# A two-layer diffusion trunk on one core: the latents' tables beside the context's mixer, layer 1's preparations behind it, and one tile's V rows summed on TensorE

## The chip, the core and the metric

One core of a Trainium2 chip (trn2) runs the whole program. The metric is the time of one execution in device microseconds (us); lower is better. The core has five engines that each work through a list of instructions of their own, in a fixed order, and wait for each other by semaphores: TensorE (PE in the profile; its weight loads are PEld), VectorE (DVE), ScalarE (ACT), GpSimd (POOL) and SyncE (SP). DMA transfers are issued by SP (all plain ones here) and by POOL (the gathers and a few loads), and run on 16 DMA engines.

## The reference

Two layers, each a token mixer and then a PEER feed-forward block, on 512 latent tokens and 256 context tokens of width 1024. In layer 0 the context is updated too; layer 1 needs the context only as input.

```python
for layer in range(2):
    y, yc = token_mixer(modulate(rms_norm(x)), modulate(rms_norm(xc)), ...)   # attention, Hyena, S5, gated merge
    x = x + g1 * y
    x = x + g2 * peer_ffn(modulate(rms_norm(x)), wq, sub_keys, u_tab, v_tab)
    if layer == 0:
        xc = xc + mc2 * yc
        xc = xc + mc5 * peer_ffn(modulate(rms_norm(xc)), wq, sub_keys, u_tab, v_tab)

def peer_ffn(x, ...):                       # 8 heads, 128 x 128 = 16384 experts, 16 chosen per head and token
    s = einsum('thsk,hsnk->thsn', x @ wq, sub_keys)       # scores against two halves of the key
    best, expert = top 16 of the sums of the two halves' top 16
    act = gelu(einsum('td,thkd->thk', x, u_tab[expert]))
    return einsum('thk,thkd->td', softmax(best) * act, v_tab[expert])
```

## The kernel before

Each part of the work is a Python generator that emits instructions and yields a cost; `weave` takes several of them, each with a factor, and always advances the one whose sum of cost times factor is least. A factor is thus a pace: a greater one means fewer steps in the same stretch. The order that comes out is fixed at build time for each engine, and an engine whose next instruction waits holds up all that stand behind it. Layer 0's middle is one such weave and then a second, smaller one.

The first weave holds five chains. (1) The context's mixer (`ctx_rest`, banks `pm`): attention, Hyena, S5, merge; its end is marked "c1". Behind it in the same chain comes `ctx_side`: the context's norm, its scores (16 projections) and for each of its two tiles of 128 tokens the pick of 128 experts per token (`peer_pick`, all on VectorE: maxima, indices, one-hot sums), after which ids and weights stand ready ("ids", q). (2) `peer_u` (banks `pu`): 128 **U tiles**, each of which loads 512 KB of the U table, splits it into a high and a low part (`wh` on ScalarE, `wl` on VectorE), multiplies it with all 512 latents in 24 matmuls of 512 columns and writes 256 KB of activations to memory. It runs until "tabs" is marked, in groups of eight; U tiles that are then left are done in the V stage. Its factor is 10 until "c1", 1.2 after it. (3) `aside` (banks `ps`): the latents' norm, layer 1's preparations `s5_prep` and `hy_prep`, the latents' scores, and for the four latent tiles a pick and then a dense gate table (`peer_table`: one-hot matrices `ohA`, `ohB` on VectorE, matmuls, 1 MB writes `ge`). When the fourth table is out it marks "tabs". (4) `gather`: for each context tile, 128 indirect DMAs of 128 rows of U (tile `gx`, 512 KB each, issued by POOL), each followed by one dot product on VectorE (L1198), then 128 gathers of V rows, each followed by one multiply-and-add on VectorE (L170). It needs the pool "gx", which `aside` opens after "c1". Its factor is 1.69. (5) `mods`, layer 1's modulation vectors, whose matmuls have 32 output rows and stand four side by side in one bank.

The second weave is the **V stage**: `peer_v` (banks `pa`, `px`) takes 128 steps; each loads 512 KB of the V table and 256 KB of activations, reads a share of the gate tables, splits both factors and does 24 matmuls of 512 columns. What is left of `gather` runs beside it with the factor 1.5; what is left even then goes on beside layer 1.

## Time and profile before

| | |
|---|---|
| median of the runs shown (3) | 5627.69 us (5614.76 to 5642.93) |
| the profiled execution's own time | 5628.3 us |
| its span, first to last instruction | 5626.4 us |
| busy over the span: PE, DVE, ACT, POOL | 87%, 66%, 31%, 26% |
| mean granted clock of TensorE | 0.932 of 2.4 GHz |
| DMA over the span | 1333.39 MB, 237 GB/s |

Busy shares are unions of an engine's instructions in time. The clock has two levels, 1.2 and 2.4 GHz; a mean between them says what share of the time stood at which. "DMA share" is the mean busy share of the 16 DMA engines. The context's mixer stands at about 890 to 1530 us of the span, the rest of the first weave reaches to 2545, the V stage to 3412, layer 1 to the end.

### The profile page before, as it was taken

How to read it: one execution, taken by the hardware profiler on the slowest of the kernel's cores; microseconds unless marked ns; L12 is line 12 of the kernel's file. 1: busy time of each engine (PE TensorE's matmuls, PEld its weight loads, DVE VectorE, ACT ScalarE, POOL GpSimd, SP SyncE). 2: the span in 40 equal slices, each digit the busy share in tenths (PEclk: the TensorE clock that was granted, in tenths of full speed). 3: DMA queues.
4: the chain of work that ended last, by engine and by line, in shares of the span. 5: the costliest groups of instructions: out<-in, count | busy, mean ns of one | idle time of the engine just before them, and what ended most of it. 6: DMA issues, size and time to landing. Idle time of an engine off the chain costs nothing.

```text
span 5626.4 us, 72472 instructions
## 1 busy us (share of the span) xinstructions
PE 4889.1 (87%) x25801; PEld 4010.3 (71%) x25801; DVE 3728.4 (66%) x7594; ACT 1758.3 (31%) x2651; POOL 1442.0 (26%) x1626
## 2 busy tenths in 40 slices
PE   6888878869997889998888887999889899998886
PEld 5666557648886777786766676875578899897665
DVE  5643426644499899987777775544345989776777
ACT  3221524314442322332222224334233333332322
POOL 0003500000002344443444441406000111243333
PEclk9899989879998999999989998999899999999998
DMA  6557335666556889899999896562444676788897
GB/s 208 190 186 262 110 111 179 206 200 189 184 175 207 303 280 325 312 329 343 324 321 321 311 308 219 174 216 75 144 148 154 214 255 240 261 311 297 310 320 257
DMA packets 641795, 1333.39 MB, mean 237 GB/s; under 512 B 56438, under 2 KB 342391, under 8 KB 626329
## 3 DMA queue, kind: packets, MB, share of 16 engines
q1 hardware_dynamic: 522776, 871.53, 47.2%
q0 software_dynamic: 118656, 457.23, 23.0%
q8 instruction: 203, 3.33, 0.2%
q14 instruction: 160, 1.30, 0.1%
HBM read 1147.01 MB, written 181.49 MB: 236 GB/s over the span
## 4 chain that ended last, share of the span: by engine, by line
PE 26%; DMA 14%; DVE 12%; issue 9%; POOL 4%; ACT 1%; SPq 1%; DVEq 0%; POOLq 0%; ACTq 0%
PE pa L181 6%; PE ps L181 5%; PE two L181 5%; DMA gx<-in_peer_v_dram,t 3%; POOL gx L1185 3%; DMA va<-t 3%; PE pu L181 3%; PE px L181 3%; PE pm L181 2%; PE pf L181 2%; DMA gt<-t 2%; DMA t<-ge 2%; DVE t L170 2%; DVE wl L160 2%; DMA x<-in_peer_v_dram 1%
## 5 line engine op out<-in xcount | busy, mean ns | idle before, releaser
L160 DVE TENSOR_TENSOR wl<-w,wh 128x1024 fp32r<-128x1024 f32 (+1 forms) x550 | 639.9, 1165 | 586.9 <-ACT wh L176 576.8
L176 ACT CAST wh<-w 128x1024 fp32r<-128x1024 f32 (+1 forms) x550 | 546.2, 994 | 1526.0 <-PE pu L181 337.0
L1185 POOL DMA_INDIRECT gx<-in_peer_un_dram,t x384 | 534.1, 1391 | 1600.3 <-DVE t L1198 777.9
L181 PE MATMUL pa<-xl,vwh 128*128 128x512 f32 x1664 | 677.2, 407 | 141.8 <-DVE xl L160 141.3
L1185 POOL DMA_INDIRECT gx<-in_peer_v_dram,t x384 | 553.6, 1442 | 797.5 <-DVE t L170 695.9
L181 PE MATMUL pa<-xh,vwh 128*128 128x512 f32 x1664 | 668.6, 403 | 40.8 <-ACT xh L176 35.0
L181 PE MATMUL pu<-t,wh 128*128 128x512 f32 x2048 | 659.0, 403 | 30.4 <-ACT ua L173 22.6
L181 PE MATMUL pa<-xh,vwl 128*128 128x512 f32 x1664 | 668.2, 402 | 0.1
L181 PE MATMUL pm<-t,wh 128*128 128x384 f32 (+1 forms) x2432 | 580.3, 325 | 9.0 <-ACT wh L176 9.0
L170 DVE SCALAR_TENSOR_TENSOR t<-gx,t,t 128x1024 f32<-128x1024 f32 x381 | 487.9, 1280 | 32.0 <-DMA gx<-in_peer_v_dram,t 30.5
L181 PEld LDWEIGHTS pa<-xl,vwh 128*128 128x128 f32 x1664 | 324.4, 195 | 235.7 <-DVE xl L160 169.1
L1198 DVE CUSTOM_DVE_ANT_0 gx<-gx,t 128x1024 f32<-128x1024 f32 x384 | 463.8, 1221 | 35.1 <-DMA gx<-in_peer_un_dram,t 35.0
L181 PEld LDWEIGHTS pu<-t,wh 128*128 128x128 f32 x2048 | 389.7, 194 | 113.3 <-ACT ua L173 27.1
L181 PE MATMUL pu<-t,wl 128*128 128x512 f32 x1024 | 413.0, 404 | 60.3 <-DVE wl L160 60.1
L181 PEld LDWEIGHTS pm<-t,wh 128*128 128x128 f32 x2432 | 426.4, 193 | 18.1 <-ACT wh L176 12.9
L181 PE MATMUL pm<-t,wl 128*128 128x384 f32 (+1 forms) x1216 | 394.1, 325 | 33.2 <-DVE wl L160 33.1
L181 PEld LDWEIGHTS pa<-xh,vwh 128*128 128x128 f32 x1664 | 323.7, 195 | 120.5 <-ACT xh L176 45.8
L176 ACT CAST vwh<-gt 128x512 fp32r<-128x512 f32 (+1 forms) x256 | 145.3, 568 | 740.6 <-PE pa L181 663.9
L181 PEld LDWEIGHTS pa<-xh,vwl 128*128 128x128 f32 x1664 | 324.8, 195 | 68.7 <-DVE vwl L160 1.3
L176 ACT CAST xh<-x 128x1024 fp32r<-128x1024 f32 x256 | 268.4, 1048 | 322.2 <-DMA x<-in_peer_v_dram 261.7
L160 DVE TENSOR_TENSOR xl<-x,xh 128x1024 fp32r<-128x1024 f32 x256 | 312.6, 1221 | 39.8 <-ACT xh L176 39.6
L160 DVE TENSOR_TENSOR gt<-va,gt 128x512 f32<-128x512 f32 (+1 forms) x256 | 155.0, 622 | 263.2 <-DMA gt<-t 134.9
(371 smaller groups left out, 9147.1 us busy)
## 6 DMA issues: line engine op xcount, KB each, us to landing
w<-in_peer_u_dram SPq DMA_DIRECT2D x256, 512.0 KB
x<-in_peer_v_dram SPq DMA_DIRECT2D x256, 512.0 KB
w<-in_in_w_dram SPq DMA_DIRECT2D x128, 512.0 KB
t<-ge SPq DMA_DIRECT2D x56, 1024.0 KB
gt<-t SPq DMA_DIRECT2D x112, 512.0 KB
w<-in_mod_w_dram SPq DMA_DIRECT2D x96, 512.0 KB
dft<-in_dft_dram POOLq DMA_DIRECT2D x32, 1024.0 KB
t<-ua SPq DMA_DIRECT2D x128, 256.0 KB
```

The costliest lines, as they stand in the source:

```text
L160: return (e or self.nc.vector).tensor_tensor(out=out, in0=a, in1=b, op=op)
L170: self.nc.vector.scalar_tensor_tensor(out=out, in0=a, scalar=s, in1=b, op0=op0, op1=op1)
L176: self.nc.scalar.copy(h, x)
L181: self.nc.tensor.matmul(out, l, r, start=start, stop=stop)
L1185: self.nc.gpsimd.indirect_dma_start(out=g, out_offset=None, in_=src, in_offset=bass.IndirectOffsetOnAxis(ap=ids[:, k:k + 1], axis=0))
L1198: self.nc.vector.tensor_tensor_reduce(out=g, in0=g, in1=x, scale=1.0, scalar=0.0, op0=OP.mult, op1=OP.add, accum_out=dot[:, c:c + 1])
```

## The change

- `aside` computes the latents' scores first and goes straight on to picks and tables; layer 1's preparations come after "c1", behind the first table, with the factor 0.6 (before: first of all, at 0.8). The pool "gx" opens at the same place, before the preparations.
- `peer_u`'s factor before "c1" is 6 and not 10.
- `gather` does only the U rows of the context's tile 0 and marks "dot"; then it goes on with tile 1 as before. Its factor in the V stage is 2.4 and not 1.5.
- The V rows of tile 0 are summed in `ctx_side` by the new `summed`: ids and weights are transposed, so that a gather of 128 rows belongs to one token (its 128 experts) and not to one expert slot of 128 tokens. A matmul with a stationary matrix of 128 x 32 that holds that token's weights in one column, and zeros, adds the token's sum into its row of the bank; four tokens of different 32-row quarters go side by side. Eight buffers `gv` hold the rows; a group of four is used four gathers after its own were issued. The two accumulators `acc` take two of the `pm` banks until the end.
- `mods` is marked as done inside the weave; `ctx_side` waits for that mark and for "dot" before it sums.

```diff
@@ -1190,7 +1190,49 @@
                     use(k - lag, made.pop(0))
             yield 1.6
-    def peer_gather(self, pool, l, j, x, p, ids, dot, src, put):
+    def summed(self, pool, src, ids, w, lane):
+        nc = self.nc
+        p = self.bank(lane)
+        f = self.t(pool, [128, 128], tag="gi", bufs=1)
+        nc.vector.tensor_copy(f, ids)
+        nc.tensor.transpose(p[:, 0:128], f, self.ident)
+        nc.tensor.transpose(p[:, 128:256], w, self.ident)
+        it = self.t(pool, [128, 128], I32, tag="git", bufs=1)
+        nc.vector.tensor_copy(it, p[:, 0:128])
+        wt = self.t(pool, [128, 4, 32], tag="gi", bufs=1)
+        nc.vector.tensor_copy(wt.rearrange("p g s -> p (g s)"), p[:, 128:256])
+        acc = [self.bank(lane) for _ in range(2)]
+        lag, made = 8 - 4, []
+        for n in range(128 + lag):
+            if n < 128:
+                t = 32 * (n % 4) + n // 4
+                g = self.t(pool, [128, D], tag="gv", bufs=8)
+                nc.gpsimd.indirect_dma_start(out=g, out_offset=None, in_=src,
+                                             in_offset=bass.IndirectOffsetOnAxis(ap=it[:, t:t + 1], axis=0))
+                made.append(g)
+            if n % 4 == (lag - 1) % 4:
+                s = (n - lag - 3) // 4
+                if s >= 0:
+                    if s % 4 == 0:
+                        z = self.t(pool, [128, 4, 4, 32], tag="gz", bufs=2)
+                        nc.vector.memset(z, 0.0)
+                        nc.vector.tensor_copy(z.rearrange("p g s c -> p g (s c)")[:, :, s:s + 100:33], wt[:, :, s:s + 4])
+                    rows = [made.pop(0) for _ in range(4)]
+                    one = lambda c, q: nc.tensor.matmul(acc[c][32 * q:32 * q + 32, :], z[:, q, s % 4, :], rows[q][:, c * 512:(c + 1) * 512],
+                                                        start=s == 0, stop=s == 31)
+                    first = one(0, 3)
+                    with self.tc.issue_after(first.ins):
+                        for c in range(2):
+                            for q in range(3, -1, -1):
+                                if c or q < 3:
+                                    one(c, q)
+                yield 6.4
+        return acc
+    def peer_gather(self, pool, l, j, x, p, ids, dot, src, put, key=None):
         w = p[:, 2].rearrange("p h k -> p (h k)")
@@ -1207,6 +1249,9 @@
         yield from self.gathered(pool, self.a["peer_un"], ids, product)
         self.act(dot, dot, AF.Gelu_apprx_tanh)
         self.tt(w, w, dot, OP.mult)
+        if key:
+            self.done.add(key)
+            return
         yield from self.gathered(pool, self.a["peer_v"].rearrange("l e d -> (l e) d"), ids, add)
         y = self.t(pool, [128, D], tag="gx", bufs=4)
         self.nc.sync.dma_start(y, src)
@@ -1480,9 +1525,7 @@
         def aside():
             yield from self.norm_to(hs[0], x1, vec[0, 1], 0, True)
             self.done.add("h")
-            yield from self.s5_prep(1, self.S[1], True)
-            yield from self.hy_prep(1, TL, self.K[1, TL], True)
-            self.done |= {("hy", 1), ("room", 1)}
+            yield from self.scores(0, hs[0], sc)
             with self.pool("pg", True) as pg, ExitStack() as ex:
                 hn, w, dot = ([self.t(pg, [128, n]) for _ in range(2)] for n in (D, 3 * 128, 128))
                 ids = [self.t(pg, [128, 128], I32) for _ in range(2)]
@@ -1490,17 +1533,20 @@
                 C.update({q: (hn[q], pc[q], ids[q], dot[q]) for q in range(2)})
                 self.done.add("pg")
                 pk = [self.t(pg, [128, 3, 8, 16]) for _ in range(2)]
-                yield from self.scores(0, hs[0], sc)
                 for q in range(5):
                     if q < 4:
                         yield from self.pick(0, sc[q], pk[q % 2])
                     if q:
                         yield from self.table(pk[(q - 1) % 2], G[q - 1])
-                    if q == 4 and "gx" not in C:
+                    if q == 3 and "gx" not in C:
                         yield from until("c1")
                     if "c1" in self.done and "gx" not in C:
                         C["gx"] = ex.enter_context(self.pool("gx", True))
-                        self.done.add("gx")
+                        self.done |= {"gx", "prep"}
+                        yield from self.s5_prep(1, self.S[1], True)
+                        yield from self.hy_prep(1, TL, self.K[1, TL], True)
+                        self.done -= {"prep"}
+                        self.done |= {("hy", 1), ("room", 1)}
                 self.done.add("tabs")
                 yield from self.stop("tables")
                 yield from until("c2")
@@ -1516,11 +1562,23 @@
             for q in range(2):
                 yield from self.pick(0, scC[q], C[q][1], C[q][2], False)
                 self.done.add(("ids", q))
+            with self.pool("gv") as gv:
+                yield from until("dot", ("mods", 1))
+                x, w, ids, _ = C[0]
+                acc = yield from self.summed(gv, a["peer_v"].rearrange("l e d -> (l e) d"), ids, w[:, 2].rearrange("p h k -> p (h k)"), "m")
+                g = self.rows(gv, 0, 1, 5, "gv", 8)
+                y = self.t(gv, [128, D], tag="gv", bufs=8)
+                nc.sync.dma_start(y, c1[0])
+                for c in range(2):
+                    k = slice(c * 512, c * 512 + 512)
+                    self.tt(x[:, k], acc[c], g[:, k], OP.mult)
+                self.tt(x, x, y, OP.add)
+                nc.sync.dma_start(c2[0], x)
         def gather():
             for q in range(2):
                 yield from until(("ids", q), "gx")
-                yield from self.peer_gather(C["gx"], 0, 1, *C[q], c1[q], lambda x: nc.sync.dma_start(c2[q], x))
+                yield from self.peer_gather(C["gx"], 0, 1, *C[q], c1[q], lambda x: nc.sync.dma_start(c2[q], x), None if q else "dot")
             self.done.add("c2")
         side, gather = aside(), gather()
@@ -1528,15 +1586,14 @@
             hs.append(self.halves(ha, TL))
             with self.psum(m=4, u=2, s=2), self.pool("ua") as ua:
                 weave((chain(self.ctx_rest(0, xc, c1, vec[0, 0], st[0]), mark("c1"), ctx_side()), lambda: 1.1 if "c1" in self.done else 1.0, "m"),
-                      (chain(until("h"), self.peer_u(0, ua, hs[0], TL, lambda i: act[i], "tabs"), mark("u")), lambda: 1.2 if "c1" in self.done else 10.0, "u"),
-                      (part(side, "tables"), lambda: 1.25 if "c1" in self.done else 1.23 if "pg" in self.done else 0.8, "s"),
-                      (self.while_(gather, "tabs"), 1.69, "s"), (mods(1, range(6), 0, 1), 1.26, "m"))
-            self.done.add(("mods", 1))
+                      (chain(until("h"), self.peer_u(0, ua, hs[0], TL, lambda i: act[i], "tabs"), mark("u")), lambda: 1.2 if "c1" in self.done else 6.0, "u"),
+                      (part(side, "tables"), lambda: 0.6 if "prep" in self.done else 1.25 if "c1" in self.done else 1.23 if "pg" in self.done else 0.8, "s"),
+                      (self.while_(gather, "tabs"), 1.69, "s"), (chain(mods(1, range(6), 0, 1), mark(("mods", 1))), 1.26, "m"))
             with self.pool("pv", True) as pv:
                 vl = self.peer_v(0, pv, hs[0], lambda i: act[i], G, x1, self.store(x2), 0)
                 next(vl)
                 with self.psum(a=7, x=1):
-                    weave((vl, 1.0, "m"), (gather, 1.5, "s"))
+                    weave((vl, 1.0, "m"), (gather, 2.4, "s"))
         self.done.add("tables")
```

**In the program's order.** On VectorE, in the Hyena part of the context's mixer (`hy`, `hz`, `hyl` are the mixer's own products), layer 1's S5 preparation (`cmp`, `cmq`, `X`) stands between them before:

```order
1080 L160 TENSOR_TENSOR hyl_9548<-hy_9541,hyh_9547 128x512
1081 L160 TENSOR_TENSOR cmp_9615<-X_9414,t_8211 128x512
1082 L160 TENSOR_TENSOR cmq_9616<-X_9414,t_8235 128x512
1083 L160 TENSOR_TENSOR X_9414<-cmp_9615,cmq_9616 128x2x16x16
1084 L160 TENSOR_TENSOR hy_9593<-pm_9569,hk_9567 128x512
1085 L160 TENSOR_TENSOR hz_9594<-pm_9569,hk_9567 128x512
1086 L160 TENSOR_TENSOR hy_9593<-hy_9593 128x256
```

With the change the first latent tile's pick (`s`, `i`, `mr` of `scin`) stands there:

```order
935 L160 TENSOR_TENSOR hyl_9794<-hy_9787,hyh_9793 128x512
936 L1054 MATCH_REPLACE mr_9840<-s_2033_9570,scin_9746 128x128
937 L1052 MAX s_2033_9570<-scin_9966 128x8
938 L1055 MAX s_2033_9570<-mr_9840 128x8
939 L1053 MAX_INDEX i_2034_9571<-s_2033_9570,scin_9966 128x8
940 L1056 MAX_INDEX i_2034_9571<-s_2033_9570,mr_9840 128x8
944 L160 TENSOR_TENSOR hy_9846<-pm_9815,hk_9813 128x512
945 L160 TENSOR_TENSOR hz_9847<-pm_9815,hk_9813 128x512
```

The preparations' vector work and their TensorE work have left the mixer's stretch, and pick work has come in their place.

On POOL, near the end of the first weave, the queue held one gather after another of a single context tile before. These are with the change the rows where tile 0's V rows (`gv`) and tile 1's U rows (`gx`) alternate:

```order
601 L1185 DMA gx_19477<-in_peer_un_dram,t_9564 128x1024
602 L1213 DMA gv_19493<-in_peer_v_dram,git_19227 128x1024
603 L1213 DMA gv_19495<-in_peer_v_dram,git_19227 128x1024
604 L1213 DMA gv_19497<-in_peer_v_dram,git_19227 128x1024
605 L1213 DMA gv_19499<-in_peer_v_dram,git_19227 128x1024
606 L1185 DMA gx_19509<-in_peer_un_dram,t_9564 128x1024
607 L1185 DMA gx_19526<-in_peer_un_dram,t_9564 128x1024
608 L1185 DMA gx_19563<-in_peer_un_dram,t_9564 128x1024
609 L1213 DMA gv_19580<-in_peer_v_dram,git_19227 128x1024
```

and these are rows of before at the turn from U rows to V rows, where all gathers go into the four `gx` buffers:

```order
836 L1185 DMA gx_24736<-in_peer_un_dram,t_11163 128x1024
837 L1185 DMA gx_24776<-in_peer_un_dram,t_11163 128x1024
838 L1185 DMA gx_24824<-in_peer_v_dram,t_11163 128x1024
839 L1185 DMA gx_24826<-in_peer_v_dram,t_11163 128x1024
840 L1185 DMA gx_24866<-in_peer_v_dram,t_11163 128x1024
```

Two streams with buffers of their own now share one queue, four rows of V to two or three of U.

On TensorE, in the same stretch, a U tile, one group of the sum (eight matmuls, four for each half of the 1024 columns) and two groups of a gate table follow each other with the change:

```order
8310 L181 MATMUL pu_19927<-t_7724,wh_19922 128x512
8311 L181 MATMUL pu_19927<-t_7723,wl_19923 128x512
8312 L1224 MATMUL pm_19231<-gv_19843,gz_19673 32x512
8313 L1224 MATMUL pm_19231<-gv_19841,gz_19673 32x512
8314 L1224 MATMUL pm_19231<-gv_19839,gz_19673 32x512
8315 L1224 MATMUL pm_19231<-gv_19837,gz_19673 32x512
8316 L1224 MATMUL pm_19232<-gv_19843,gz_19673 32x512
8320 L181 MATMUL ps_19978<-ohB_19905,ohA_19904 128x128 x4
8321 L181 MATMUL ps_19997<-ohB_19972,ohA_19971 128x128 x4
8322 L181 MATMUL pu_20012<-t_7723,wh_20007 128x512
```

Before, the same place holds `pu` and `ps` alone. TensorE's own queue now stands behind the landing of gathers.

Counted in this order: with the change 120 of the 128 U tiles stand in the first weave, and 8 in the V stage. Ahead of the V stage VectorE does 199 dot products (before 128) and no V add (before 103); TensorE sums the 128 V rows of tile 0 there. In the V stage itself there are 57 dot products and 125 V adds (before 128 and 145), and 2 adds are left behind it (before 5). "c1" falls behind U tile 9 (before behind U tile 5), the first sum behind U tile 87.

## Rows read from the trace of the kernel before

**Rows 1.** Windows of the context's mixer. The columns are named in the first line.

```profile
core 0: us, PE busy (x) PEld busy (x) DVE busy (x) ACT busy (x) POOL busy (x), PEclk, DMA share, GB/s
963.00:1063.00 100.00, 87.03 (x538) 60.02 (x538) 75.67 (x250) 37.40 (x79) 2.18 (x4) 0.84 0.64 206
1063.00:1163.00 100.00, 78.43 (x550) 65.30 (x550) 65.10 (x110) 24.65 (x36) 0.00 (x0) 0.83 0.66 212
1163.00:1263.00 100.00, 67.05 (x353) 41.02 (x354) 38.52 (x67) 15.09 (x21) 1.59 (x3) 0.79 0.69 183
1263.00:1363.00 100.00, 92.51 (x657) 84.50 (x656) 45.44 (x67) 45.17 (x69) 8.59 (x11) 0.99 0.66 207
1363.00:1463.00 100.00, 100.00 (x677) 92.14 (x676) 39.32 (x48) 44.86 (x65) 7.43 (x8) 1.00 0.51 155
1463.00:1530.00 67.00, 66.84 (x422) 59.89 (x420) 27.02 (x36) 24.84 (x31) 2.32 (x2) 1.00 0.62 200
```

**Rows 2.** Windows of the later stretches: first weave, V stage, layer 1's V stage.

```profile
1530.00:2065.00 535.00, 455.74 (x2262) 378.20 (x2263) 481.78 (x1612) 169.24 (x250) 123.84 (x94) 0.94 0.70 234
2065.00:2306.00 241.00, 218.16 (x1070) 181.12 (x1069) 226.86 (x551) 71.80 (x105) 101.95 (x74) 0.97 0.87 309
2306.00:2545.00 239.00, 225.56 (x1204) 193.46 (x1202) 204.43 (x369) 79.09 (x123) 98.06 (x67) 0.98 0.92 334
2545.00:3412.00 867.00, 745.41 (x3072) 601.02 (x3072) 641.01 (x800) 203.28 (x256) 383.79 (x275) 0.92 0.93 320
4900.00:5100.00 200.00, 200.00 (x1016) 182.05 (x1015) 148.84 (x216) 70.39 (x96) 96.98 (x62) 1.00 0.87 305
```

**Rows 3.** DMA queues, 2166 to 2545 us: packets, MB, share of 16 engines.

```profile
q1 hardware_dynamic: 22442, 62.41, 45.7%
q0 software_dynamic: 15670, 57.03, 42.6%
...
w<-in_peer_u_dram SPq DMA_DIRECT2D x46, 512.0 KB
```

**Rows 4.** DMA queues of the V stage, 2545 to 3412 us.

```profile
q1 hardware_dynamic: 99450, 133.32, 48.0%
q0 software_dynamic: 39456, 143.67, 44.6%
```

**Rows 5.** Chain that ended last, pieces: start us, us, what.

```profile
2097.76 5.46 PE pu L181 x24
...
2236.57 8.67 DMA gx<-in_peer_v_dram,t
```

**Rows 6.** VectorE groups, 1530 to 2545 us: busy us, mean ns, idle before.

```profile
L160 DVE TENSOR_TENSOR wl<-w,wh 128x1024 fp32r<-128x1024 f32 x139 | 169.6, 1220 | 25.8 <-ACT wh L176 25.8
L1198 DVE CUSTOM_DVE_ANT_0 gx<-gx,t 128x1024 f32<-128x1024 f32 x128 | 155.0, 1220 | 21.9 <-DMA gx<-in_peer_un_dram,t 21.9
L167 DVE TENSOR_SCALAR ohA<-t,pt 128x128 f32<-128x128 f32 x512 | 143.8, 352 | 0.0
L170 DVE SCALAR_TENSOR_TENSOR t<-gx,t,t 128x1024 f32<-128x1024 f32 x102 | 130.8, 1283 | 8.4 <-DMA gx<-in_peer_v_dram,t 7.7
L160 DVE TENSOR_TENSOR ohB<-t,pt 128x512 f32<-128x512 f32 x128 | 88.1, 688 | 8.2 <-PE ps L181 8.2
...
L1198 DVE DVE_READ_ACCUMULATOR2_ANT t<- 128x1 f32 x128 | 10.9, 85 | 0.0
```

**Rows 7.** VectorE groups, 963 to 1300 us: layer 1's S5 preparation.

```profile
L160 DVE TENSOR_TENSOR X<-cmp,cmq 128x512 f32<-128x512 f32 x32 | 21.9, 685 | 15.5 <-PE ps L181 15.2
L160 DVE TENSOR_TENSOR cmq<-X,t 128x512 f32<-128x512 f32 x28 | 19.2, 685 | 0.0
```

**Rows 8.** TensorE groups, 963 to 2545 us: modulation, table, latents' score matmuls.

```profile
L181 PE MATMUL ps<-ohB,ohA 128*128 128x128 f32 x1024 | 134.0, 281 | 23.6 <-ACT ge L1141 14.6 <-DVE ohA L167 9.0
L181 PE MATMUL ps<-t,wh 128*128 128x512 f32 x256 | 79.5, 392 | 0.0
...
L181 PE MATMUL pm<-w,t 128*32 128x256 f32 x320 | 33.0, 437 | 4.8 <-DMA w<-in_mod_w_dram 4.8
```

## The prediction

> **What bounds the kernel now.** I read the windows first, stretch by stretch, then the DMA queues, then the listing of groups for prices. The change touches the span from 963 us (where the first U tile starts) to 3412.
>
> In the windows of the context's mixer [rows 1] the reader is to see two halves. From 963 to 1263 TensorE is busy 87, 78 and 67% at granted clocks of 0.84, 0.83 and 0.79 of 2.4 GHz: multiplied, 191 us of full-clock work in 300 us. From 1263 on it is busy 92 to 100% at 0.99 to 1.00. The first half is short of ready work, the second is bound by TensorE.
>
> In the later stretches [rows 2] the reader is to see which share is nearest to one. From 1530 to 2306 it is VectorE (481.78 of 535 us, then 226.86 of 241, 94%). From 2306 to 2545 VectorE (86%), TensorE (94%) and DMA (0.92) are close together. In the V stage it is DMA: 0.93 over 867 us at 320 GB/s, while TensorE is busy 86% at a clock of 0.92. The last row, from layer 1's V stage, shows TensorE at 100% and full clock with DMA at 0.87, so TensorE can be fully fed if DMA stays a little below its limit.
>
> That limit is worked out from the queues. In the late first weave [rows 3] 62.41 MB took 45.7% of 379 us, which is 360 GB/s at a full share, and the gathers 57.03 MB in 42.6%, which is 353; I use 355. In the V stage [rows 4] the gathers have 143.67/(0.446 x 867) = 372, the plain loads 320.
>
> **Prices.** 24 matmuls of 512 columns last 5.46 us, 0.2275 each [rows 5]. On VectorE [rows 6] a split is 1.22 us, a dot product 1.22 + 0.085 = 1.305, a V add 1.283, a gate table (143.8 + 88.1)/4 = 58. The six rows sum to 698; VectorE was busy 913 there (sum over three windows [rows 2]), so the six picks are the rest, 36 us each. Layer 1's preparations: the two rows shown [rows 7] give 41 us, a third operation like the second 19, the small ones I estimate at 35: 95. A gather moves 128 rows of 4 KB, 0.524 MB, like a table load [rows 3].
>
> **Part by part**, in the program's order with the change. A stretch gets the largest of its engine sums, divided by 0.94, the share that VectorE reached where it was the bound.
>
> *Mixer, to "c1".* Behind U tile 9 now. Up to U tile 3 the order holds 190 us of TensorE work at the prices above: the latents' 384 score matmuls (87 us; the kind in [rows 8]), three U tiles (16), and 87 of the mixer's own. This is dense, 190/0.94 = 202. From there to U tile 6 stand Hyena's and S5's outputs, 83 us of TensorE beside two picks (72) and some 48 us of other vector work: at best 120/0.94 = 128, and at the density of the first half now (64%) 83/0.64 = 130 for TensorE alone, up to 180 if the mixer's loads wait as they do today. I take 150. Then gates, merge and the first table's start: 127 of TensorE, 135. Together 487 us for 567 now: **-80**. The preparations that leave cost nothing here, since they are priced below.
>
> *"c1" to "dot" (U tiles 10 to 86).* First the context's scores: 13 U tiles (71), 46 of projections, 26 of table and rest on TensorE, 143/0.94 = 152. Then 41 splits (50), 73 dot products (95), three picks (108), half a table (29) and 80 of the preparations, 362 of VectorE: 385. Then 23 splits (28), 53 dots (69), 42 of tables, one pick (36): 175, so 186. Together 723.
>
> *"dot" to the V stage.* The order has 34 U tiles here. DMA: 40 MB of table loads, activations and gate tables, 73 gathers for dots (38.3 MB) and the 128 V rows (67.1 MB), 145.4 MB: 410 us at 355 GB/s. TensorE: 186 of U tiles, 60 of gate tables (134.0/128 = 1.05 a group), 12 of others, and the sum. For the sum, the modulation's matmuls show the price: 320 records of 256 columns busy 33.0 us, 0.103 each, though one lasts 437 ns [rows 8]. They run four abreast. A group of four is eight records, 0.83 us; at 512 columns double, 64 groups are 106 us. From below, 128-column records at the gate table's 134.0/1024 = 0.131 give 0.52 for 512 columns, two passes a group: 67. I take 67, and keep 106: TensorE 325 to 364. VectorE: 37 splits, 73 dots, 103 of tables, some 12 for weights and zeros of the sum: 255. The 102 V adds that left would have been 131. So DMA is the bound, 410/0.94 = 436, and TensorE's added work hides behind it by over 70 us; without that cover it would cost its 67 to 106.
>
> The first weave is then 487 + 723 + 436 = 1646 us, against 1582 now: **+64**. The cause is 96 gathers more ahead of the V stage (50 MB, 142 us), less what the mixer and VectorE give back.
>
> *V stage.* 182 uses of gathers for 273; 91 gathers are 48 MB. DMA: 135 MB of plain loads at 320 GB/s and 95 MB at 372 are 679 us. TensorE: 128 steps and 8 U tiles, 136 x 5.46 = 743, now the larger. 743/0.94 = 790, against 867: **-77**. Leaving 2 adds for layer 1 rather than 5 is nothing.
>
> Sum: -80 + (723 + 436 - 1015) - 77, with 1015 us for 1530 to 2545 today, is -13. From the profiled execution's own 5628.3 us (2 above its span, within 1 of the median) that is **5615 us**.
>
> **What a page adds.** The Trainium skill, "DMA: Bandwidth & Descriptors", section Specifications, gives two ceilings, 435 GB/s for the fabric and about 358 for one core's share of HBM. By the first the tail would be 145.4/0.435/0.94 = 356 and the sum 5535. The trace's 353 to 360 agrees with the second, which leaves the sum as it is. The Trainium skill, "TensorEngine Tiling", section Key Properties, says that changing the tiling mode drains TensorE, which speaks against 32-row groups among full ones. No row here shows the drain by itself; by that rule, some 66 changes come on top of the sum's price, and they too lie under DMA's cover.
>
> **Rivals.** *A, within 0.5% (my forecast):* 5600 to 5656. Tail and mixer cancel. Chance 0.36.
>
> *B, faster:* the mixer's short half was starved by the preparations alone, and the V stage runs as layer 1's fused steps do [rows 2]. Then the middle piece takes 120 and the dense ones run at 97%, 445 us in all (-42), and the V stage 753 (-37): 5536. For it speaks that the preparations' 95 us of VectorE work, and their loads, stood between the mixer's own instructions; against it that two picks now stand there. Chance 0.33 with its milder forms, below 5600.
>
> *C, slower:* the sum's gathers head TensorE's queue. If a group of four only lands once the group before it is done, each of 32 cycles costs TensorE's 325/32 = 10 us plus a landing, 8.67 [rows 5]: 600 us, not 436, and 5779. It decides once the last row of a group lands over 3.5 us after TensorE is ready for it (436/32 less 10). For it: POOL issues `gv` behind `gx` gathers that wait for VectorE. Against: eight buffers, two groups ahead. Chance 0.25, mostly in part.
>
> *D, the four don't run abreast:* 64 groups cost four times 67 to 106, TensorE's tail becomes 526 to 682 us, and the time 5720 or more. Against it stands the modulation [rows 8]. Chance 0.06.
>
> **How the numbers follow.** Some 0.5%, 28 us, is about what a measurement of this kernel tells from no change. The bounds: mixer -42 to +45, middle 25 either way, tail 410 to 480, V stage 755 to 820. Taken together as independent they give about 65 either way, 5550 to 5680; C in part pulls the upper end to 5715, and B sets the lower at 5545. Faster 0.33, same 0.36, slower 0.31 (C and D).
>
> **What would show it.** "c1" near 1450 us (wrong if past 1500). From U tile 10 to 86 VectorE at 90% or more. From "dot" to the V stage a DMA share over 0.9 and TensorE at 60 to 75%: a share under 0.85 there, with TensorE waiting for `gv`, is C. In the V stage TensorE over 90% busy, 6 us a step or less, DMA below 0.9. The `gv` matmuls' busy time should be a quarter of count times duration, or D holds. The forecast is wrong above all if the tail leaves its 436 us, or the mixer its 487.

## The result and the profile after

The changed kernel takes 5663.32 us (median of 5 runs, 5634.83 to 5668.96) against 5626.48 for the kernel before on the same chip: ratio 1.0051, 95% interval 1.0031 to 1.0071. It is slower by 17 to 40 us, where the prediction had it 13 us faster. The time lies in the predicted range, but the sign of the sum is wrong, and errors of the parts cancel in it (below).

The profiled execution took 5634.83 us, the fastest of the five, and its span is 5633.0 us. A second profile of the same kernel (the run again, below) has a span of 5645.9, against 5626.4 before. So the stages below show 7 to 20 us of a loss that the two ratios put at 29 to 38; the rest is in executions that no profile shows.

The windows of after, in the prediction's stretches (columns as in [rows 1]); the first three answer [rows 1], the others [rows 2]:

```profile
972.00:1186.00 214.00, 204.02 (x1269) 157.41 (x1268) 84.32 (x195) 83.30 (x138) 2.18 (x4) 0.99 0.61 192
1186.00:1363.00 177.00, 127.13 (x818) 98.55 (x817) 123.49 (x471) 48.80 (x69) 4.76 (x4) 0.87 0.56 161
1363.00:1486.00 123.00, 121.46 (x951) 117.86 (x950) 95.86 (x169) 64.27 (x90) 10.07 (x12) 1.00 0.63 198
1486.00:1639.00 153.00, 152.76 (x959) 133.68 (x958) 107.62 (x302) 70.47 (x119) 0.00 (x0) 1.00 0.68 219
1639.00:2047.00 408.00, 328.52 (x1482) 265.38 (x1481) 345.49 (x1039) 100.30 (x139) 102.48 (x82) 0.87 0.70 237
2047.00:2243.00 196.00, 166.18 (x771) 135.97 (x770) 177.62 (x496) 53.52 (x78) 74.90 (x56) 0.92 0.80 282
2243.00:2639.00 396.00, 327.03 (x1832) 227.45 (x1831) 231.88 (x489) 88.30 (x136) 228.68 (x201) 0.93 0.99 390
2639.00:3451.00 812.00, 757.26 (x3216) 616.70 (x3214) 546.42 (x653) 209.19 (x265) 280.51 (x183) 0.97 0.85 284
```

The reader is to see three stretches with three bounds. In the fifth, VectorE is the bound by the prediction, but it is busy only 85%. In the seventh DMA stands at 0.99, at 390 GB/s. In the eighth, the V stage, TensorE is busy 93% and DMA has fallen to 0.85.

The DMA view of the same tail (first the share in tenths and GB/s in 40 slices, then the queues); it answers [rows 3]:

```profile
DMA  7899899999999999999999999999999999978979
GB/s 271 282 410 419 275 419 419 419 421 418 417 422 415 420 419 418 419 420 415 420 416 419 420 416 422 419 420 392 372 417 396 412 424 415 418 290 295 326 244 337
...
q0 software_dynamic: 28889, 105.17, 67.0%
q1 hardware_dynamic: 17846, 49.05, 32.0%
```

Most slices move 415 to 422 GB/s. The same working as the prediction's, bytes over the queue's share of the time, gives 396 here for the gathers (105.17 MB in 67.0%) and 387 for the plain transfers. So the 355 that it took from [rows 3], where the shares add up to 0.88, was not the limit.

Waits, first in the mixer's middle piece, then in the stretch of tile 0's dot products (1747 to 2246 us), then in the tail (2243 to 2632; who waits <- for what: us, times, longest):

```profile
ACT y L173 <- DVE y L160: 42.0, 4, 19.7
DVE y L160 <- PE pm L181: 26.2, 6, 6.6
PE pm L181 <- DMA t<-t: 25.6, 4, 14.7
ACT wh L176 <- DMA w<-in_glu_w_dram: 20.0, 2, 18.9
...
PE pu L181 <- DVE wl L160: 58.3, 12, 39.6
ACT fst L671 <- PE ps L181: 47.6, 8, 11.5
POOL dft L676 <- PE ps L181: 22.6, 7, 4.9
...
PEld pm L1224 <- DMA gv<-in_peer_v_dram,git: 63.1, 15, 10.8
```

The mixer's middle waits for its own products and loads, with the preparations gone. In the second piece TensorE stands 39.6 us in one go at the first dot products (25.0 in before), and POOL, which issues the gathers, waits for TensorE in the preparations. In the tail TensorE waits for V rows.

### The profile page after: what moved, and what is told of

It reads as the page before. It is cut to its first block, busy times and chain, and to the rows that moved or that the text cites. A ratio compares the mean times of both kernels' runs of the same rounds, so it can differ in the third digit from the quotient of the medians.

```text
span 5633.0 us, 73131 instructions
## 1 busy us (share of the span) xinstructions
PE 4931.0 (88%) x26315; PEld 3998.6 (71%) x26315; DVE 3592.4 (64%) x7495; ACT 1765.6 (31%) x2657; POOL 1408.3 (25%) x1626
## 4 chain that ended last, share of the span: by engine, by line
PE 38%; DMA 17%; DVE 15%; issue 7%; ACT 2%; POOL 2%; SPq 1%; DVEq 0%; ACTq 0%; POOLq 0%
PE pa L181 10%; PE ps L181 7%; PE pm L181 6%; PE pu L181 5%; PE two L181 4%; PE px L181 3%; DMA gt<-t 3%; DMA va<-t 3%; DVE wl L160 2%; PE pf L181 2%; DMA gv<-in_peer_v_dram,git 2%; DMA t<-ge 2%; DVE gx L1240 2%; DVE xl L160 1%; DVE t L170 1%
## 5 line engine op out<-in xcount | busy, mean ns | idle before, releaser
L181 PE MATMUL pu<-t,wh 128*128 128x512 f32 x1920 | 628.4, 407 | 18.8 <-ACT ua L173 15.5
L1185 POOL DMA_INDIRECT gx<-in_peer_v_dram,t x256 | 383.0, 1496 | 699.4 <-DVE t L170 646.7
L1240 DVE CUSTOM_DVE_ANT_0 gx<-gx,t 128x1024 f32<-128x1024 f32 x384 | 462.2, 1217 | 76.0 <-DMA gx<-in_peer_un_dram,t 68.2
L181 PEld LDWEIGHTS pu<-t,wh 128*128 128x128 f32 x1920 | 367.9, 195 | 109.6 <-ACT ua L173 20.3
L181 PE MATMUL pu<-t,wl 128*128 128x512 f32 x960 | 389.4, 407 | 58.9 <-DVE wl L160 58.9
L170 DVE SCALAR_TENSOR_TENSOR t<-gx,t,t 128x1024 f32<-128x1024 f32 x254 | 324.7, 1278 | 4.7 <-DMA gx<-in_peer_v_dram,t 4.7
```

The lines of the kernel that those rows point to most:

```text
L170: self.nc.vector.scalar_tensor_tensor(out=out, in0=a, scalar=s, in1=b, op0=op0, op1=op1)
L181: self.nc.tensor.matmul(out, l, r, start=start, stop=stop)
L1185: self.nc.gpsimd.indirect_dma_start(out=g, out_offset=None, in_=src, in_offset=bass.IndirectOffsetOnAxis(ap=ids[:, k:k + 1], axis=0))
L1240: self.nc.vector.tensor_tensor_reduce(out=g, in0=g, in1=x, scale=1.0, scalar=0.0, op0=OP.mult, op1=OP.add, accum_out=dot[:, c:c + 1])
```

## The ledger

One number per stretch makes the kernels comparable: TensorE's lack, the length less busy time times PEclk. The stretches are cut at the first U tile, the context's first key scores, the first and the 128th dot product, the V stage's first and last matmul and layer 1's first. The windows of after, cut so:

```profile
972.00:1522.00 550.00, 488.61 (x3245) 404.95 (x3245) 332.32 (x902) 221.46 (x338) 17.00 (x20) 0.95 0.61 189
1522.00:1747.00 225.00, 219.55 (x1245) 187.76 (x1244) 169.54 (x527) 79.15 (x123) 5.17 (x4) 0.96 0.57 182
1747.00:2246.00 499.00, 394.92 (x1772) 318.93 (x1773) 435.50 (x1245) 122.44 (x172) 174.62 (x135) 0.88 0.78 271
2246.00:2639.00 393.00, 324.03 (x1811) 224.66 (x1810) 228.91 (x483) 85.91 (x133) 226.27 (x200) 0.93 1.00 392
2639.00:3445.00 806.00, 755.93 (x3211) 615.95 (x3210) 540.88 (x645) 209.19 (x265) 280.51 (x183) 0.97 0.85 284
3445.00:3492.00 47.00, 23.57 (x123) 17.55 (x123) 33.26 (x59) 29.91 (x52) 0.00 (x0) 0.64 0.55 197
```

The same cuts in before (the two that differ most; its dot products' stretch is the second):

```profile
964.00:1561.00 597.00, 517.82 (x3336) 424.56 (x3336) 306.32 (x600) 210.44 (x331) 22.11 (x28) 0.91 0.62 192
1749.00:2171.00 422.00, 345.96 (x1661) 286.51 (x1660) 392.58 (x1072) 113.64 (x167) 170.62 (x127) 0.92 0.82 290
```

Length and lack in us, worked out so for the kernels before and after and for four experiments, told below (again is the changed kernel once more; all six stretches, then the sum):

| | mixer | scores | tile 0's dots | to V stage | V stage | behind it | sum |
|---|---|---|---|---|---|---|---|
| before | 597, 126 | 188, 7 | 422, 104 | 374, 39 | 863, 178 | 60, 45 | 2504, 498 |
| no_sum | 555, 87 | 225, 14 | 506, 159 | 279, 38 | 894, 183 | 91, 73 | 2550, 555 |
| sum_only | 598, 129 | 187, 6 | 427, 103 | 469, 64 | 782, 83 | 46, 31 | 2509, 417 |
| preps_first | 656, 154 | 176, 8 | 451, 92 | 422, 80 | 787, 94 | 45, 30 | 2537, 457 |
| after | 550, 86 | 225, 14 | 499, 151 | 393, 92 | 806, 73 | 47, 32 | 2520, 448 |
| again | 552, 85 | 224, 14 | 501, 154 | 396, 95 | 810, 80 | 49, 34 | 2532, 461 |

With the change the lack falls by 50 us, but TensorE's work grows by 66 (from 2504 - 498 to 2520 - 448), as the sum's own 71 us (below) would have it. The mixer's lack falls by 40 us and that of tile 0's dot products rises by 47.

## The experiments

Two theories stood first. Theory 1: the loss comes from the gathers brought ahead of the V stage. Theory 2: it comes from the new order. Every ratio is to the kernel before on the same chip, with its 95% interval.

**The change again, unchanged** (again).

> The changed kernel once more, nothing edited. The profiled execution of it took 5634.8 us, the median of its five 5663.3, so its stretches understate the median by some 28 us. If that is spread over all stretches, the end of the mixer, the start of the V stage and the start of layer 1's V stage shift in proportion; if one stretch has two lengths, one of them moves by 20 us or more. Median 5650 to 5670, ratio 1.003 to 1.007.

1.0067 (1.0047 to 1.0087), 5666.4 us: the loss is real.

**The two halves of the change.** no_sum leaves `summed` out, so that both tiles gather and add as before:

```diff
-            with self.pool("gv") as gv: ...
-                ..., None if q else "dot")
+                ...)
-                    weave((vl, 1.0, "m"), (gather, 2.4, "s"))
+                    weave((vl, 1.0, "m"), (gather, 1.5, "s"))
```

> The changed kernel without the sum on TensorE: both context tiles gather and add as before, V stage factor 1.5 as before; the new order of tables and preparations and the U factor 6 stay. Theory 1 (the loss is in bringing 96 gathers forward into the first weave; the new order gains its 44 us in the mixer): 5585 to 5610, ratio 0.993 to 0.997. Theory 2 (the loss is in the order: picks hold up the mixer, preparations beside the first dot products leave VectorE idle): 5640 to 5670, ratio 1.003 to 1.008.

sum_only keeps the sum and its factor 2.4, with before's order:

```diff
+            yield from self.s5_prep(1, self.S[1], True)      # ahead of self.scores(0, hs[0], sc) again
-  ... else 6.0, "u")
+  ... else 10.0, "u")
-  lambda: 0.6 if "prep" in self.done else 1.25 ...
+  lambda: 1.25 ...
```

> The kernel before with the sum on TensorE and the V stage factor 2.4 alone; preparations first, U factor 10, as before. Theory 1: 5640 to 5675, ratio 1.003 to 1.009, first weave longer by 30 us or more than the V stage is shorter. Theory 2: 5585 to 5615, ratio 0.993 to 0.998.

no_sum: 1.0052 (1.0036 to 1.0069), 5660.8 us. sum_only: 0.9993 (0.9977 to 1.0009), 5622.1 us. The new order, with its pace of 6 for the U tiles, is the whole loss; the sum alone changes nothing that can be measured, so theory 1 falls. The V stage of sum_only, with the stretch ahead of it:

```profile
2175.00:2644.00 469.00, 421.50 (x2252) 305.95 (x2250) 338.63 (x825) 115.58 (x171) 277.60 (x232) 0.96 1.00 394
2644.00:3426.00 782.00, 728.15 (x3070) 593.27 (x3070) 502.70 (x576) 202.83 (x256) 228.92 (x149) 0.96 0.82 273
```

The sum adds 95 us ahead of the V stage (469 for 374, at a DMA share of 1.00), and takes 81 from it (782 for 863) and 14 behind it (46 for 60).

**Do the picks hold the mixer up?** late_picks holds them until "c1":

```diff
+                yield from until("c1")
                 for q in range(5):
```

> The changed kernel with the picks of the latent tiles held back until the context's mixer has ended; scores and U tiles stay beside the mixer. If the picks hold up the mixer on VectorE, its end falls from 1486 us to 1455 or earlier. If it is the mixer's own loads, it stays within 10 us of 1486. Either way two picks and the first table move behind it, 100 us of VectorE's work where VectorE is the bound, so the time is 5700 to 5740, ratio 1.013 to 1.02.

1.0279 (1.0259 to 1.0299), 5783.5 us, over the 5740 expected. Without the picks the mixer's second half takes 292 us (from 1188 to 1480), with them 300 (1186 to 1486 above):

```profile
1188.00:1480.00 292.00, 238.38 (x1655) 205.64 (x1656) 165.75 (x403) 103.42 (x143) 12.88 (x16) 0.89 0.58 171
```

So the picks cost the mixer some 8 us. Moved behind it they cost over 100.

**Where the preparations stand.** preps_last moves `s5_prep` and `hy_prep` behind the last gate table, just ahead of "tabs"; preps_first moves them alone back ahead of the scores (the pace of 6 and the rest of the new order stay); preps_slow changes their factor alone, by the edit shown first:

```diff
-  lambda: 0.6 if "prep" in self.done else 1.25 if "c1" ...
+  lambda: 1.25 if "c1" ...
```

bare_new and bare_old leave them out of the change and of sum_only (layer 1 then uses layer 0's tables, so the output is not the reference's):

```diff
+        self.S = [self.S[0], self.S[0]]
+        self.K[1, TL] = self.K[0, TL]
-                        yield from self.s5_prep(1, self.S[1], True)
-                        yield from self.hy_prep(1, TL, self.K[1, TL], True)
```

> The changed kernel with layer 1's preparations moved once more: behind the last gate table, just ahead of "tabs". Theory 2 (the dot products' chain sets the end of layer 0, and the preparations beside it hold it up): their 95 us of VectorE work leave the stretch from the first dot product to "dot", VectorE is busy 90% there instead of 85%, "dot" comes 40 to 80 us sooner, and the time is 5590 to 5640 us. Rival (the work of the first weave is only shifted: what leaves one stretch costs the same in the next, where DMA is at 0.99): 5645 to 5690 us, as the change itself.

> The changed kernel with layer 1's preparations put back ahead of the latents' scores, all else as changed (U factor 6.0, the dot products' room from the fourth pick on, the sum). If the preparations beside the dot products are what the new order loses by, the time is that of sum_only, 5612 to 5635 us. Rival (the other moved work, or the U tiles' pace): 5650 to 5675 us, as the change.

> The changed kernel with the preparations at the tables' pace (factor 1.25 instead of 0.6). If their bursts at the head of VectorE and SP make the stall at the first dot products (TensorE idle for 39 us at 1745, 25 us in before) it falls to about 25 us and the time to 5640 to 5656 us. Rival (their pace does not matter, or what is late then is the last table): 5660 to 5690 us.

> The changed kernel with layer 1's preparations left out (layer 1 uses layer 0's tables of the same shape in their place). If the preparations' place is what costs, their price behind "c1" is 65 to 95 us: 5570 to 5600 us against the change's 5663 to 5666. Rival (other moved work costs it): 5610 to 5640 us.

> sum_only (before's order and the sum, 5622 us) with layer 1's preparations left out in the same way. If they lie in the mixer's slack there, their price is 10 to 30 us: 5592 to 5612 us, that is above bare_new. Rival (they cost the same in either place, and the other moved work makes the difference): 5540 to 5575 us, some 40 us below bare_new.

preps_last: 1.0175 (1.0162 to 1.0188), 5720.5 us. preps_first: 1.0040 (1.0025 to 1.0056), 5655.8. preps_slow: 1.0115 (1.0093 to 1.0137), 5692.5. bare_new: 1.0037 (1.0023 to 1.0050), 5654.8. bare_old: 0.9978 (0.9963 to 0.9992), 5621.2. preps_first met its rival: with the preparations back in their old place most of the loss stays. The other four lie outside both of their ranges. In preps_slow TensorE's long stall at the first dot products is gone (its longest wait for `wl` in tile 0's stretch is 7.6 us for 39.6), yet the time rises, so that stall by itself is not the loss. Tile 0's dot products in preps_last and in bare_new, in each with what follows up to the V stage; for bare_new the V stage as well, and below it that of bare_old:

```profile
1725.00:2178.00 453.00, 381.92 (x1799) 314.18 (x1800) 413.25 (x1126) 121.48 (x180) 169.39 (x126) 0.91 0.82 284
2178.00:2716.00 538.00, 393.98 (x1955) 274.54 (x1954) 264.41 (x554) 91.49 (x134) 232.18 (x208) 0.83 0.85 311
```

```profile
1734.00:2183.00 449.00, 378.73 (x1804) 311.27 (x1803) 412.84 (x1126) 123.28 (x182) 169.97 (x127) 0.92 0.82 287
2183.00:2481.00 298.00, 184.07 (x960) 90.32 (x959) 74.30 (x158) 32.07 (x49) 150.17 (x147) 0.80 0.91 327
2481.00:3414.00 933.00, 889.30 (x3789) 726.79 (x3789) 622.40 (x780) 248.09 (x313) 326.48 (x217) 0.97 0.81 270
```

```profile
2487.00:3414.00 927.00, 881.41 (x3789) 720.63 (x3790) 622.56 (x764) 248.94 (x313) 326.96 (x217) 0.98 0.81 272
```

What is shown: in every profile with the preparations beside tile 0's dot products (after, again, no_sum and seven more) these take 487 to 517 us (late_picks, which has picks there too, 549), and in the nine that have neither them nor late picks there, 422 to 459. They cost this stretch some 50 us (499 in after, 449 in bare_new): VectorE has 23 us more work there (435.50 for 412.84) and is idle 27 us more. The other 27 of the 77 us by which the stretch grew over before's 422 are there without any preparations. TensorE lacks 151 to 159 us there in after and no_sum, and 92 to 105 in before, sum_only, preps_first, preps_last and bare_new. But whoever takes them away does not get these 50 us: in preps_first TensorE lacks 154 us in the mixer for after's 86; in preps_last they stand ahead of "tabs", without which the first weave does not end, and the V stage is 538 us away; and without them altogether "tabs" comes when 96 U tiles are done, in bare_new and in bare_old, so that the V stage takes the other 32, and 933 and 927 us. So theory 2 holds for the stretch and fails for the sum: the price of the preparations in the whole, 8 to 17 us in the change and 8 in sum_only (differences of the ratios), is far below what it is in their stretch. And without any preparations the changed order still takes 0.59% more than the old one (bare_new against bare_old), as much as after against sum_only: at the pace of 6 most of the loss does not hang on where they stand.

**The pace of the U tiles.** Theory 2, extended, had U tiles in the way of the scores behind "c1"; theory 4 (its number in the expectations), formed after it failed, had layer 0 last as long as TensorE's work and lack, so that U tiles in the mixer's lack are time won. One factor each, u_slow, u_ten and u_three in the change, sum_u_slow and sum_u_five in sum_only:

```diff
-  lambda: 1.2 if "c1" in self.done else 6.0
+  lambda: 1.2 if ("ids", 0) in self.done else 4.0 if "c1" in self.done else 6.0     # u_slow; sum_u_slow: else 10.0
+  lambda: 1.2 if "c1" in self.done else 10.0     # u_ten; u_three: 3.0; sum_u_five: 5.0
```

> The changed kernel with U tiles at a third of their pace between "c1" and the moment at which the context's first picks are there (factor 4.0 instead of 1.2), then as before. Theory 2, extended (between "c1" at 1486 us and the first dot product at 1747 TensorE is full, 256 of 261 us, and 27 U tiles, 147 us, stand among the context's scores on which the dot products wait): the first dot product comes at about 1650 to 1700 us and the time falls to 5600 to 5640 us. Rival (TensorE's own sum sets the end): the U tiles come back later and the time stays at 5645 to 5685 us.

> The order of before with TensorE's sum (the run sum_only) and the U tiles held to a third of their pace between "c1" and the context's first picks. Theory 2, extended: the first dot product comes 40 to 80 us ahead of 1748 us and the time is 5570 to 5605 us, below both kernels. Rival (TensorE's own sum sets the end): 5610 to 5640 us, as sum_only's 5622.

> The changed kernel with before's pace of the U tiles ahead of "c1": factor 10.0 instead of 6.0. Theory 4 (layer 0 lasts as long as TensorE's work and its idle time; U tiles done while the mixer leaves TensorE free are time won): some 4 or 5 U tiles less stand at "c1", their 5.46 us each come back behind it, and the time is 5675 to 5695 us against the change's 5663 to 5666. Rival (theory 2, extended: U tiles hold up the mixer, and with it the scores and dot products): "c1" comes 25 us sooner and the time is 5635 to 5655 us.

> The changed kernel with the U tiles at double their pace ahead of "c1": factor 3.0 instead of 6.0. Theory 4: U tiles fill part of the 71 us that TensorE lacks between 1186 and 1486 us; 6 to 10 more of them stand at "c1", which comes 10 to 30 us later, and the time is 5630 to 5655 us. Rival (theory 2, extended): the mixer, and all that waits for it, is held up by the added tiles' 33 to 55 us, and the time is 5680 to 5710 us.

> The order of before with TensorE's sum (the run sum_only, 5622 us) and the U tiles at double pace ahead of "c1": factor 5.0 instead of 10.0. Theory 4: U tiles fill part of the 112 us that TensorE lacks between 963 and 1279 us, and the time is 5590 to 5612 us, below both kernels. Rival (theory 2, extended): the mixer is held up, 5630 to 5660 us.

u_slow: 1.0111 (1.0096 to 1.0125). sum_u_slow: 1.0055 (1.0041 to 1.0069). u_ten: 1.0088 (1.0068 to 1.0109). u_three: 1.0121 (1.0099 to 1.0143). sum_u_five: 1.0047 (1.0029 to 1.0066). In sum_u_slow the dot products do start 38 us sooner (1710 for 1748), but TensorE idles among the scores:

```profile
1554.00:1710.00 156.00, 116.17 (x669) 99.31 (x668) 148.11 (x704) 47.06 (x73) 4.64 (x4) 0.90 0.47 147
```

It lacks 51 us there for 6 in sum_only, and 16 U tiles go over into the V stage. In u_three and sum_u_five more U tiles stand ahead, but the mixer, and with it the first dot product, is late: 1800 and 1782 us. Both theories fail as rules: a faster pace and a slower one both lose, in either order, though u_ten's loss against again (1.0088 and 1.0067) is within the intervals. The mixer of sum_only (pace 10) and of sum_u_five (pace 5), of bare_old (10) and bare_new (6), of u_ten (10):

```profile
963.00:1561.00 598.00, 515.34 (x3335) 427.05 (x3335) 306.67 (x600) 210.65 (x332) 21.65 (x28) 0.91 0.62 192
967.00:1594.00 627.00, 554.51 (x3534) 456.86 (x3535) 314.01 (x606) 232.79 (x356) 21.19 (x28) 0.93 0.62 193
```

```profile
982.00:1499.00 517.00, 453.80 (x2977) 371.64 (x2976) 300.78 (x831) 195.31 (x304) 19.55 (x20) 0.94 0.60 184
984.00:1537.00 553.00, 491.71 (x3244) 405.21 (x3243) 332.05 (x902) 221.56 (x338) 17.06 (x20) 0.95 0.61 187
```

```profile
976.00:1503.00 527.00, 460.74 (x3073) 383.23 (x3073) 322.61 (x894) 201.37 (x315) 17.92 (x20) 0.93 0.60 186
```

The faster pace makes the mixer longer each time: 627 for 598, 553 for 517, and 550 in after for u_ten's 527. In before's order this is not won back: the pace alone, 5 for 10, costs 0.54% (sum_u_five, 1.0047, against sum_only, 0.9993). Two less clean pairs, in which the latents' scores also run at the factor 0.8 and not 1.23 and the tables wait for "c1" one pick earlier, agree: preps_first against sum_only 0.47%, bare_new against bare_old 0.59%. At the pace of 10 the preparations behind "c1", with the scores and picks ahead of it, cost 0.95% (u_ten against sum_only). Both together cost 0.6 to 0.7%: the two losses do not add, and at the pace of 6 the place of the preparations is worth only 0.1 to 0.3% (after and again against preps_first), which is within the intervals.

**What bounds the tail.** twice makes each of the sum's matmuls twice (each row counts twice), half_sum gathers and sums the rows of only 64 of the 128 tokens (not 64 rows of each token, as its expectation says; the bytes are the same), and sum_hold and hold move the gathers of 45 and 31 dot products into the V stage:

```diff
+                        for r in range(2):                     # twice
-        for n in range(128 + lag):
+        for n in range(64 + lag):                              # half_sum
-  (self.while_(gather, "tabs"), 1.69, "s")
+  (self.while_(gather, "tabs"), lambda: 3.0 if "dot" in self.done else 1.69, "s")   # sum_hold, hold
-  (gather, 2.4, "s")
+  (gather, 1.9, "s")                                           # sum_hold, hold
```

> The changed kernel with every matmul of the sum of V rows made twice (its result counts each row twice). By the prediction the sum lies under the transfers' cover in the stretch from "dot" to the V stage: the time stays within 15 us of the change's, 5650 to 5680 us. Rival (TensorE is on the path there): its own time a second time, 67 to 106 us by the prediction's bounds, 5730 to 5770 us.

> The changed kernel with only 64 of the 128 rows of V gathered and summed for each token (half of the sum is left out): 33.6 MB and 256 matmuls less between "dot" and the V stage. If the transfers bound that stretch, it gets up to 33.6 MB at 391 GB/s, 86 us, shorter, and the time is 5580 to 5600 us. If TensorE does, it gets half of the sum's 71 us shorter, and the time is 5625 to 5640 us. If neither (VectorE's dot products and tables), 5650 to 5670 us.

> sum_only with the dot products' gathers at just over half their pace once "dot" is done (factor 3.0 instead of 1.69) and 1.9 instead of 2.4 in the V stage: by the order of the instructions 186 instead of 231 dot products stand ahead of the V stage. Theory 5 (after "dot" transfers are the bound at about 391 GB/s; the V stage has transfers to spare): 45 gathers, 23.6 MB, up to 60 us less ahead of the V stage, 30 us more in it at 0.67 us a use (from 152 uses in 782 us and 273 in 863), and the time is 5585 to 5610 us, below both kernels. Rival (the V stage pays as much as the first weave gains): 5615 to 5640 us.

> The changed kernel with the same two factors: 168 instead of 199 dot products ahead of the V stage. Theory 5: 31 gathers, 16.3 MB, up to 42 us less ahead of the V stage, 21 us more in it, 5635 to 5655 us. Rival: 5658 to 5685 us.

twice: 1.0109 (1.0094 to 1.0123), 5682.8 us. half_sum: 0.9922 (0.9901 to 0.9943), 5584.1 us. sum_hold: 1.0002 (0.9986 to 1.0019). hold: 1.0056 (1.0038 to 1.0073). The windows of the sum's own instructions (`gv`), in after and in twice (PE, PEld, DVE and POOL busy):

```profile
2246.00:2639.00 393.00, 71.33 (x512) 14.27 (x512) 2.61 (x3) 140.11 (x128) 0.93 1.00 392
```

```profile
2255.00:2673.00 418.00, 125.97 (x1024) 31.48 (x1024) 2.61 (x3) 142.19 (x128) 0.95 0.95 368
```

The second pass is 54.6 us of TensorE. It makes the stretch 25 us longer, and the time 24 to 33 us (ratios against again and after), which is between the two ranges expected: the cover that the prediction claimed is there for about half of it. Half of the gathers gone, 33.6 MB, gives 73 to 82 us (ratios against after and again); at 391 GB/s they are 86, and the TensorE work that goes with them is only 36. So the tail is bound mainly by transfers, as forecast. But sum_hold takes 34 us from the stretch ahead of the V stage and pays 43 in it:

```profile
2186.00:2621.00 435.00, 407.25 (x2251) 301.84 (x2249) 284.29 (x735) 116.57 (x173) 214.97 (x188) 0.99 0.96 374
2621.00:3446.00 825.00, 736.21 (x3069) 598.42 (x3070) 552.61 (x666) 203.00 (x256) 286.63 (x194) 0.93 0.84 286
```

Theory 5 of its expectation fails: at 0.84 the V stage's DMA share leaves room, yet TensorE's lack rises from 83 to 140 us. Here a gather that was moved was paid for where it went, and one that was not made was time won.

No version beats the kernel before: sum_only is level with it, and half_sum and bare_old leave work out.

## Why the prediction was wrong, step by step

*The mixer, -80 us: this step failed first.* "c1" came at 1486 us and not near 1450, 44 sooner by the prediction's own marks and not 80. The pieces took 214, 177 and 123 us for 202, 150 and 135, and the first U tile came 9 us late. The middle piece was mis-sized most. It lies near the upper bound that the prediction named for loads that wait as today, 180; the waits listed above are 45.6 us for loads and 68.2 for the mixer's own products, and late_picks shows that it is not the picks. The U tiles ahead of "c1" were counted at their TensorE time alone, and their faster pace got no price of its own: u_ten, with the old pace, has the mixer's stretch 23 us shorter (527 for 550), and in before's order the pace alone costs 0.54%.

*"c1" to "dot", 723 us: this step failed too.* It took 757, of which the preparations' piece has 408 for 385. Its work was sized rightly (345 us of VectorE for 362), but not the share: the 0.94 at which VectorE runs [rows 2] was read off a stretch without the preparations. The preparations are chains through TensorE, ScalarE, POOL and DMA. With them VectorE is busy 87% of tile 0's stretch, against 93% of before's (435.50 of 499, 392.58 of 422): of 77 us more, 43 are work and 34 idle time. The preparations' own part, against bare_new, is 50 us: 23 of work and 27 of idle time. The prediction read the preparations as 95 us of vector work and priced no wait of theirs.

*"dot" to the V stage, 436 us: right bound, wrong limit.* 396 us, with a DMA share of 0.99, as forecast over 0.9; but at 390 GB/s and not 355 x 0.94 = 334, and with 154.55 MB where 145.4 had been worked out. TensorE was busy 83%, over the 60 to 75% forecast (the prediction's own 325 to 364 of 436 us are 75 to 83%); the sum is 71 us, near the lower bound of 67 that was taken. The four run abreast, so D falls: a quarter of 512 times 592 ns is 76 us, and the busy time is 71. The listing of these matmuls (ns: least, median, greatest):

```profile
L1224 PE MATMUL pm<-gv,gz x512: 592/592/1063, 2278.8 to 2621.1; 128*32 128x512 f32 x171
```

*V stage, 790 us: 812.* TensorE at 93% and DMA at 0.85 are as forecast. Its queues, which answer [rows 4], moved 230 MB where the prediction had worked out 230:

```profile
q1 hardware_dynamic: 98721, 134.12, 53.2%
q0 software_dynamic: 26352, 95.96, 31.3%
```

Only the steps were mis-sized. The 8 steps that do a U tile too took 83 us (2639 to 2722), 10.4 each, the other 120 took 729, 6.07 each, for 5.81 forecast (5.46/0.94).

*Five adds or two behind it: nothing.* Layer 1's first matmul comes 47 us behind the V stage's last and not 60. It is 13 us, and 31 the other way in no_sum (91).

Together: the first weave ends at 2639 and not 2609 (963 and 1646), the V stage takes 22 more: +52 us on -13 is +39. Of the 52, the mixer with its late start has 36, "c1" to "dot" 34 and the V stage 22, and the tail, 40 us short of its forecast, hid as much. The two steps of the new order, 70 us, turn the sign; the tail's error is luck, without which the time would lie some 40 us higher, near the upper end of the range. The profiled execution gets 32 of that back behind the V stage (from 3451 it has 2182 us left, before 2214 from 3412), 13 of it the adds; the rest is not explained.

*Rivals.* B, faster, rested on preparations that starved the mixer alone; the mixer's lack did fall by 40 us (126 to 86), and came back among the dot products (104 to 151). C is in part true: TensorE waits 63.1 us for V rows in the tail, the longest 10.8, but 15 times in all, and not a landing for each of 32 cycles.

*What a page adds.* The Trainium skill, "DMA: Bandwidth & Descriptors", section Specifications, has 358 GB/s as one core's share; this trace contradicts it as a limit, with 390 over 396 us. The Trainium skill, "Perfetto Trace Analysis", section Roofline, says that a core that runs alone can go above that share, up to some 435 GB/s, and with this the slices of 415 to 422 agree. The prediction weighed the wrong one of two figures; it would have had the tail at 356 us by the other and still have missed the loss.

**What stays open.** Why moved work is paid for almost in full wherever it goes is argued and not shown: from the tables that end the first weave, which decide how many U tiles the V stage takes (128 in the first weave of sum_only, 120, 112 and 96 in after, u_ten and bare_new), and from three bounds that follow each other. bare_old, level with sum_only, has only 96 there too, so their number alone decides nothing. That a faster pace costs before's order 0.54% is shown by one edit; why is argued from the longer mixer and the first dot product's delay (1782 us in sum_u_five for 1748). Why the pace and the moved preparations together cost less than the sum of the two stays open.

## What to carry to other kernels

Price a moved chain of dependent work by the idle time that it brings to the bounding engine in its new place as well as by its busy time: of the 50 us that the preparations added to tile 0's dot products, 27 were waits and not work. Then test the place by leaving the work out in both orders: here that showed that most of the loss was elsewhere, and a change of the U tiles' pace by itself cost before's order about as much as the whole change. Where one order has been balanced so that stretches with different bounds follow each other, ask of every gain ahead what ends the stretch: here the end of the tables, not the end of TensorE's work, cut the U tiles off. And take a transfer limit from slices with a full share, not from a stretch whose share is below one.

## What the hardware showed

DMA moved 415 to 422 GB/s in most slices of a 396 us stretch, while indirect gathers of 4 KB rows took 67.0% of the engines' time; in before, 353 to 360 had been worked out for the same kinds from a stretch with a share of 0.88. A token's row of the sum costs 0.56 us of TensorE (71.33/128) when it is added once, and 0.43 (54.6/128) when the same matmuls follow once more. By the Trainium skill, "TensorEngine Tiling (Array Packing)", section Key Properties, a change of the tiling mode drains TensorE. That would fit the difference; no run here shows the drain by itself, and the granted clock of the two stretches differs too (0.93 and 0.95).
